# Rotating images by 90 degrees: the first load split in 16 and 112 partitions, in place of a wait before the first store

## The chip, the core and the metric

The kernel runs on one core of a Trainium2 chip. Its time is in microseconds on the device, the median of several executions. The core has 128 partitions of on-chip memory (SBUF), engines that compute, of which this kernel uses VectorE (DVE) and a little of ScalarE (ACT), and 16 DMA engines that move data between SBUF and the chip's main memory (HBM). SyncE (SP) issues all DMAs of this kernel, in the order of the program.

## The reference

```
batch, c, h, w = 32, 3, 256, 256
x = random normal, float32
np.rot90(x, k=-1, axes=(-2, -1))
```

So each of 96 images of 256 x 256 floats is turned by 90 degrees clockwise. Nothing is calculated: 25.17 MB are read and 25.17 MB written, and every element has a new place.

## The kernel before

The 96 images are cut into 12 slabs of 2 MB (8 images each). Each slab has a buffer of its own in SBUF, `units[n]`, of 128 partitions with 2 x 2048 floats (16 KB) on each. So all slabs fit at once, and no load ever waits for a buffer.

*Loads.* The first loop issues all loads, one after the other. Slab 0 comes in two loads of 1 MB (L70): 128 partitions with 8 KB each, that is eight image rows for each partition. Slabs 1 to 10 come in two loads of 1 MB each (L72), which have 64 partitions (every second one) and 16 KB, or 16 image rows, on each. The last slab, number 11, comes in three: 1 MB over all partitions (L64), then 0.25 MB over the first `M = P // 4` = 32 partitions (L65), which the program calls `near_end`, and 0.75 MB over the other 96 (L66). A DMA on SyncE waits, besides its own data, until the DMA eight places before it has landed: eight completion counters take turns.

*Transposes.* The second loop runs over slabs. VectorE's transpose turns blocks of 32 x 32 and writes a slab's result into the buffer of the slab before (`units[n - 1]`), which is free by then; slab 0's result goes to PSUM (`turned0`). Slabs 0 and 11 take two transposes of 128 x 2048 (L80), the others two each (L86).

*Stores.* They are issued in the same loop, on the same SyncE queue, so behind all loads in program order. The result of slab 1 goes out in three stores: 128 KB, which is the first 256 floats of each partition (L89), 896 KB (L92) and 1 MB (L93). Slabs 2 to 11 go out as stores of 2 MB (L95). Slab 0's result is copied by ScalarE from PSUM into the last slab's buffer (L98) and goes out last (L99).

*The order between them.* The first store (L89) has an added dependence on `near_end` (L65): SyncE does not issue it, nor any store behind it, until all loads but the last 96 partitions of the last slab have landed.

Of the kernel before, what the change touches and what calls it, by code (L numbers as in the profile page):

```python
# [1 line left out]

# [4 lines left out]

@with_exitstack
def kernel(
    ctx: ExitStack,
    tc: tile.TileContext,
    x: bass.AP,
    out: bass.AP,
):

    nc = tc.nc
    fp32 = mybir.dt.float32

    B, C, H, W = x.shape  # L40
    P = nc.NUM_PARTITIONS
    RI, RO = 16, 8
    K = H // RI
    I = 2
    Q = P // (K * I)
    n_slabs = B * C // (Q * I)
    last = n_slabs - 1
    F = RO * W
    M = P // 4

    rows_in = x.rearrange("b c h w -> (b c h) w")
    rows_out = out.rearrange("b c h w -> (b c h) w")
    ld8_v = rows_in.rearrange("(n i p r) w -> n p i (r w)", i=I, p=P, r=RO)
    ld16_v = rows_in.rearrange("(n i m r) w -> n i m (r w)", i=I, m=Q * K, r=RI)
    st_v = rows_out.rearrange("(n i p c) w -> n p i (c w)", i=I, p=P, c=RO)

    pools = [ctx.enter_context(tc.tile_pool(name=f"unit{u}", bufs=1)) for u in range(n_slabs)]
    units = [pool.tile([P, I, F], fp32, name=f"u{u}") for u, pool in enumerate(pools)]
    psum = ctx.enter_context(tc.tile_pool(name="psum", bufs=1, space=bass.MemoryType.PSUM))
    turned0 = psum.tile([P, I, F], fp32, name="turned0")  # L60

    for n in range(n_slabs):
        if n == last:
            nc.sync.dma_start(out=units[n][:, 0], in_=ld8_v[n][:, 0])  # L64
            near_end = nc.sync.dma_start(out=units[n][:M, 1], in_=ld8_v[n][:M, 1])  # L65
            nc.sync.dma_start(out=units[n][M:, 1], in_=ld8_v[n][M:, 1])  # L66
            continue
        for i in range(I):
            if n == 0:
                nc.sync.dma_start(out=units[n][:, i], in_=ld8_v[n][:, i])  # L70
            else:
                nc.sync.dma_start(out=units[n][i::I].rearrange("p i f -> p (i f)"), in_=ld16_v[n, i])  # L72

    for n in range(n_slabs):
        t_in, t_out = units[n], units[n - 1] if n else turned0
        if n in (0, last):
            for i in range(I):
                src = t_in[:, i].rearrange("p (r g c) -> p c r g", r=RO, c=RO)
                dst = t_out[:, i].rearrange("p (c g r) -> p c r g", c=RO, r=RO)
                nc.vector.transpose(out=dst[:, :, ::-1, ::-1], in_=src)  # L80
        else:
            src = t_in.rearrange("p i f -> p (i f)").rearrange("p (r g c) -> p c r g", r=RI, c=RO)
            dst = t_out.rearrange("p i (c k r) -> p c r k i", c=RO, r=RI)[:, :, ::-1, ::-1, :]
            for h in range(2):
                cs = slice(h * RO // 2, (h + 1) * RO // 2)
                nc.vector.transpose(out=dst[:, cs], in_=src[:, cs])  # L86

        if n == 1:
            first = nc.sync.dma_start(out=st_v[n][:, 0, :W], in_=t_out[:, 0, :W])  # L89
            tc.add_manual_dep(first.ins, near_end.ins.name, mybir.DependencyInfo(  # L90
                mybir.DependencyClass.Sync, mybir.DependencyReason.DATA), reason="stores after loads")
            nc.sync.dma_start(out=st_v[n][:, 0, W:], in_=t_out[:, 0, W:])  # L92
            nc.sync.dma_start(out=st_v[n][:, 1], in_=t_out[:, 1])  # L93
        elif n:
            nc.sync.dma_start(out=st_v[n], in_=t_out)  # L95

    for i in range(I):
        nc.scalar.copy(out=units[last][:, i], in_=turned0[:, i])  # L98
    nc.sync.dma_start(out=st_v[0], in_=units[last])  # L99


# [1 line left out]
_INS = ['x']  # L103
_OUTS = [((32, 3, 256, 256), 'float32')]


# [23 lines left out]
```

## Time and profile before

| What | us |
|---|---|
| Median of 3 runs (125.41 to 126.25) | 125.93 |
| The profiled execution's own time | 126.25 |
| Its span, from the first to the last instruction | 124.5 |
| VectorE busy, 24 instructions | 93.3 |
| of it the transposes of L86, 20 of 3.945 | 78.0 |
| ScalarE busy, 3 instructions | 5.0 |
| A 1 MB load (L70, L72, L64), median from issue to landing | 19.6 |
| The loads of 0.25 MB (L65) and 0.75 MB (L66), issue to landing | 19.3 and 19.4 |
| The first store of 128 KB (L89), issued at 61.84, issue to landing | 2.9 |
| A 2 MB store, median from issue to landing | 22.0 |
| Packets of all DMAs, as a share of 16 engines' span | 98.1% |

All times that say "at" count from the start of the span. From issue to landing a DMA mostly waits in the DMA engines' queues behind those issued before it. The rows by stretches give, for each stretch of time, how long each computing engine was busy, the mean busy share of the 16 DMA engines and the rate at which their packets moved bytes; a packet counts in the stretch in which it starts, so that single short stretches can show a share above 1. A packet is one contiguous piece of a transfer, 8 KB for most of the transfers here.

### The profile page before, as it was taken

The numbers are of one execution on the slowest core, as the hardware profiler recorded it, in microseconds if no ns is written. First come the engines' busy times: TensorE is split into PE (matmuls) and PEld (weight loads), VectorE is DVE, ScalarE is ACT, GpSimd is POOL, SyncE is SP. The second block draws the span as 40 slices with busy tenths as digits, with TensorE's granted clock in tenths as the row PEclk, the third lists the DMA queues.
The fourth block names the chain that finished last, engine by engine and source line by source line (L and its number), as shares of the span: only waits on it lengthen the run. The fifth ranks groups of instructions, "written<-read, shape, count | busy, mean of one in ns | idle before, by whom it ended". The sixth has DMA issues, their size and how long they took to land.

```text
span 124.5 us, 137 instructions
## 1 busy us (share of the span) xinstructions
DVE 93.3 (75%) x24; ACT 5.0 (4%) x3; POOL 0.2 (0%) x4
## 2 busy tenths in 40 slices
DVE  0199999999999999999999999999999900000000
ACT  0000000000000000000400000000002350000000
POOL 0000000000000000000000000000000000000000
DMA  3999999999999999999999999999999999999995
GB/s 90 427 453 427 427 437 432 421 437 432 421 432 432 427 427 427 442 421 395 219 357 428 429 416 429 413 424 419 421 416 421 421 421 419 421 421 421 421 421 213
DMA packets 5616, 50.33 MB, mean 404 GB/s; under 512 B 624, under 2 KB 752, under 8 KB 880
## 3 DMA queue, kind: packets, MB, share of 16 engines
q1 hardware_dynamic: 5616, 50.33, 98.1%
HBM read 25.17 MB, written 25.17 MB: 404 GB/s over the span
## 4 chain that ended last, share of the span: by engine, by line
DMA 51%; DVE 13%; issue 10%; DVEq 6%; ACT 1%
DMA u<-in_x_dram 51%; DVE u L86 13%; DVEq L125 6%; ACT u L98 1%; DVE u L80 0%
## 5 line engine op out<-in xcount | busy, mean ns | idle before, releaser
L86 DVE STREAM_TRANSPOSE u<-u 128x2048 f32<-128x2048 f32 x20 | 78.0, 3945 | 0.3
L80 DVE STREAM_TRANSPOSE turned<-u 128x2048 f32<-128x2048 f32 x2 | 7.6, 3826 | 5.8 <-DMA u<-in_x_dram 5.8
L80 DVE STREAM_TRANSPOSE u<-u 128x2048 f32<-128x2048 f32 x2 | 7.7, 3953 | 0.0
L98 ACT COPY u<-turned 128x2048 f32<-128x2048 f32 x2 | 3.7, 1866 | 36.1 <-DVE u L80 36.1
L98 ACT ACT_TABLE_LOAD x1 | 1.3, 1283 | 60.2 <-DMA u<-in_x_dram 60.2
L114 POOL MEMSET const-bfloat16-1.0<- 128x1 bf16 x1 | 0.1, 102 | 0.0
L114 POOL MEMSET const-uint8-127<- 128x1 uint8 x1 | 0.1, 102 | 0.0
L114 POOL MEMSET const-float32-1.0<- 128x1 f32 x1 | 0.1, 99 | 0.0
L114 POOL MEMSET const-float32-0.0<- 128x1 f32 x1 | 0.1, 98 | 0.2 <-issue 0.2
## 6 DMA issues: line engine op xcount, KB each, us to landing
u<-in_x_dram SPq DMA_DIRECT2D x23, 1024.0 KB, 19.6
out_dram<-u SPq DMA_DIRECT2D x11, 2048.0 KB, 22.0
out_dram<-u SPq DMA_DIRECT2D x1, 1024.0 KB, 6.4
out_dram<-u SPq DMA_DIRECT2D x1, 896.0 KB, 4.4
u<-in_x_dram SPq DMA_DIRECT2D x1, 768.0 KB, 19.4
u<-in_x_dram SPq DMA_DIRECT2D x1, 256.0 KB, 19.3
out_dram<-u SPq DMA_DIRECT2D x1, 128.0 KB, 2.9
```

The lines of the kernel that those rows point to most:

```text
L80: nc.vector.transpose(out=dst[:, :, ::-1, ::-1], in_=src)
L86: nc.vector.transpose(out=dst[:, cs], in_=src[:, cs])
L98: nc.scalar.copy(out=units[last][:, i], in_=turned0[:, i])
L114: nc = _bacc.Bacc("TRN2", target_bir_lowering=False, num_devices=1)
L125: with _tile.TileContext(nc) as tc:
```

## The change

Three edits. The first load of 1 MB (slab 0's first half) becomes two loads, one of the first 16 partitions (128 KB) and one of the other 112 (896 KB). The last slab's three loads become a single one of 2 MB over all partitions, and the name `near_end` goes. The first store loses its added dependence, so it waits only for its own data and for the DMA eight places before it. Loads are 24 in place of 25. The three stores of slab 1, the transposes and the copies stay as they are.

```
-    M = P // 4
+    FIRST = 16
...
         if n == last:
-            nc.sync.dma_start(out=units[n][:, 0], in_=ld8_v[n][:, 0])
-            near_end = nc.sync.dma_start(out=units[n][:M, 1], in_=ld8_v[n][:M, 1])
-            nc.sync.dma_start(out=units[n][M:, 1], in_=ld8_v[n][M:, 1])
+            nc.sync.dma_start(out=units[n], in_=ld8_v[n])
             continue
         for i in range(I):
             if n == 0:
-                nc.sync.dma_start(out=units[n][:, i], in_=ld8_v[n][:, i])
+                for a, b in ((0, FIRST), (FIRST, P)) if i == 0 else ((0, P),):
+                    nc.sync.dma_start(out=units[n][a:b, i], in_=ld8_v[n][a:b, i])
...
         if n == 1:
-            first = nc.sync.dma_start(out=st_v[n][:, 0, :W], in_=t_out[:, 0, :W])
-            tc.add_manual_dep(first.ins, near_end.ins.name, mybir.DependencyInfo(
-                mybir.DependencyClass.Sync, mybir.DependencyReason.DATA), reason="stores after loads")
+            nc.sync.dma_start(out=st_v[n][:, 0, :W], in_=t_out[:, 0, :W])
             nc.sync.dma_start(out=st_v[n][:, 0, W:], in_=t_out[:, 0, W:])
```

## The prediction, made before the changed kernel ran

> **What bounds the kernel now.** I read the page's slices first, because they say which resource is never idle.
>
> ```profile
> DVE  0199999999999999999999999999999900000000
> ACT  0000000000000000000400000000002350000000
> ...
> DMA  3999999999999999999999999999999999999995
> GB/s 90 427 453 427 427 437 432 421 437 432 421 432 432 427 427 427 442 421 395 219 357 428 429 416 429 413 424 419 421 416 421 421 421 419 421 421 421 421 421 213
> ```
>
> A slice is 3.11 us. The DMA engines are busy from the second slice to the last, so the end is set by how fast 50.33 MB pass through them. VectorE, busy for 93.3 us, stops in slice 30, and ScalarE soon after. Three places stand out: the start (90 GB/s), the end (213), and a hole in slices 18 to 20 (395, 219, 357) where the DMA row still says 9. Against 427 the hole lacks 32 + 208 + 70 GB/s over 3.11 us each, 0.96 MB, or 2.3 us.
>
> Second, the chain of waits, which gives the pace of the loads:
>
> ```profile
> 0.73 5.01 DMA u<-in_x_dram
> ...
> 5.76 19.55 DMA u<-in_x_dram
> ...
> 25.32 19.56 DMA u<-in_x_dram
> ...
> 44.91 19.32 DMA u<-in_x_dram
> ```
>
> Each piece is one load from issue to landing, and it is issued when the load eight places before it has landed. So 19.56 us is the time of eight loads of 1 MB: 2.445 us each. The last piece holds six whole loads (the last five of L72 and that of L64) and the loads of 0.25 and 0.75 MB (L65, L66): 7 MB, which should take 17.11 us. It took 19.32, 2.2 us too much. That is the hole, seen from another side.
>
> Third, rows of half a microsecond around the start and the hole. The columns after the stretch are VectorE, ScalarE and GpSimd busy (and instructions), a clock that plays no part, the DMA share and GB/s.
>
> ```profile
> 1.50:2.00 0.50, 0.00 (x0) 0.00 (x0) 0.00 (x0) 1.00 0.91 131
> 2.00:2.50 0.50, 0.00 (x0) 0.00 (x0) 0.00 (x0) 1.00 0.19 49
> 2.50:3.00 0.50, 0.00 (x0) 0.00 (x0) 0.00 (x0) 1.00 0.92 311
> ...
> 58.00:58.50 0.50, 0.50 (x1) 0.00 (x0) 0.00 (x0) 1.00 0.99 410
> ...
> 59.50:60.00 0.50, 0.50 (x1) 0.00 (x0) 0.00 (x0) 1.00 0.93 197
> 60.00:60.50 0.50, 0.47 (x2) 0.31 (x1) 0.00 (x0) 1.00 1.17 213
> 60.50:61.00 0.50, 0.50 (x1) 0.50 (x1) 0.00 (x0) 1.00 0.95 197
> 61.00:61.50 0.50, 0.50 (x1) 0.47 (x1) 0.00 (x0) 1.00 0.95 262
> 61.50:62.00 0.50, 0.50 (x1) 0.00 (x0) 0.00 (x0) 1.00 1.00 262
> 62.00:62.50 0.50, 0.50 (x1) 0.00 (x0) 0.00 (x0) 1.00 1.15 295
> ```
>
> Share and rate give the time of one 8 KB packet, 16 x share x 8.192 / GB/s. At 58.0 it is 16 x 0.99 x 8.192 / 410 = 0.32 us. In the hole it is 0.62, 0.72, 0.63, 0.475, 0.50 and 0.51 us. So the engines are not idle in the hole: they carry slow packets, and these are exactly the packets of L65 (32 partitions, two packets for each of 16 engines, 0.62 and a like one before it) and L66 (96 partitions, six packets; the five rows from 60.0 have a mean of 0.57). Eight packets at 0.31 would be 2.5 us; these eight took about 2 x 0.63 + 6 x 0.57 = 4.7 us. The excess is 2.2 us for the third time. Loads over fewer than 128 of consecutive partitions are slow here, and the wait is not what makes the hole.
>
> Last, SyncE's waits, for the wait itself:
>
> ```profile
> SPq L89 <- DMA u<-in_x_dram: 16.5, 1, 16.5
> ```
>
> **The change, part by part.** *The wait at L89 goes.* The first store was issued at 61.84, after 16.5 us of waiting, and behind it on SyncE stood all other stores. Without the wait it goes out when the load eight places ahead has landed, near 47 us, its data having been ready since about 21 us (first L86 pair at 13.36 plus 7.8). But its packets join the engines' queues behind the loads, which are never empty: over 62.0 to 64.0 the share is 1.15, 0.72, 0.80 and 1.26, mean 0.98. A queue full of loads is the cover; I put the gain of the wait at 0, at most 0.1 us. Were the cover gone, about 1 us from issue to first byte (0.73 to some 1.75 at the start) would show. If instead stores passed ahead of loads, late loads would cost nothing until VectorE held up the stores: the last store is issued at 101.36 and lands 22.2 us later, of which it needs about 5 itself (2.1 MB at 421 GB/s), so there are 17 us to spare, and 14 for the one before it (issued at 99.5, landing near 118.6).
>
> *L64, L65 and L66 become one 2 MB load.* It covers 128 partitions in 8 KB rows, as the 2 MB stores do, which run at 421. It ends the slow packets: -2.2 us. Bounds: -1.6 if part of the hole belongs to the turn from loads to stores (the 128 KB store in 1 KB rows stays, at 62.8 to 63.5, rows of 180 and 234 GB/s), -2.3 by the slices. VectorE's L80 on the last slab now waits for 2 MB instead of 1, but starts at 91.69, some 30 us after landing. Two issues of 0.35 us less on SyncE lie under 19 us of queue.
>
> *The first 1 MB load becomes 16 + 112 partitions.* This brings slow packets to the start, where nothing covers them: every later packet of each engine queues behind. Before, 131 GB/s in 0.5 us is eight packets begun, 49 is three, 311 is 19: half the engines begin at about 1.75 and the others only after 2.5. The load landed at 5.74, though 1.75 + 8 x 0.31 + 0.5 for landing (the store's data end by 123.0, its landing is at 123.6) is 4.7: starting costs 1.0 us. After, the first load has one packet for each engine. No row shows a load of 16 partitions; 128 take 0.31 a packet, 32 take 0.62, half of 32 might double again: 1.24, with 0.31 as the other end. I take 1.24, since the nearest row is the 32 one and the fall is steep, and 0.3 more for the slow first touch that the first packets show. The load of 112 has seven packets an engine, between 0.31 (128) and 0.57 (96): 0.43, the middle, makes 3.0. In all 1.75 + 1.24 + 0.3 + 3.0 + 0.5 = 6.8, less 0.15 since all engines may begin a little earlier with so small a first load: 6.65, +0.9 us on the first landing. Low end: full-rate packets and all engines awake at 1.65, 1.65 + 0.9 + 7 x 0.31 + 0.5 = 5.2, -0.5. High end: 1.75 + 1.24 + 0.7 + 7 x 0.57 + 0.5 = 8.2, +2.4. VectorE starts later by the same amount, inside its 14 us of room; the added issue of about 0.35 us on SyncE delays the second load's issue, which has more than 4 us of queue ahead of it.
>
> The Trainium skill, "SBUF — State Buffer", section "Door 1: The DMA port swizzle", says that a DMA's rate depends on how many of 16 ports its partitions reach, and by its table 32 partitions from 0 reach eight, 16 reach four, which speaks against the new split as much as against the old one. The 0.62 us of the 32-partition packets agrees with it. An estimate from that page's table, seven consecutive partitions an engine, is 1.24 for the 16 and up to 2.8 for the 112, which would put the cost at the start at 0.7 and the time at 124.4.
>
> **Sum.** -2.2 + 0.9 = -1.3 us. The profiled execution took 126.25 (its span of 124.5 and 1.75 around it), and would take 124.95; the median of the runs is 0.3 lower, so 125.93 - 1.3 = 124.6.
>
> **Rivals.** *The start costs nothing or gains* (the small load's slow packet hides under the first touch, and 112 partitions run like 128): -2.2 - 0.5 to -2.2 + 0.1, 123.2 to 123.8. For it: first packets were slow anyway. Against: 32 and 96 were both slow on all engines. *The start takes back all*: costs of 1.6 to 2.6, 125.3 to 126.3; for it, the 96-partition mean of 0.57. *Slower*: the packets of the new first loads go at the worst row of the hole, 0.72, or 1.44 for those of 16 partitions: 1.75 + 1.44 + 0.7 + 7 x 0.72 + 0.5 = 9.4, +3.7, against -2.2: 127.4. It decides when a 112-partition packet takes more than about 0.7 us; only one row of the hole was that slow, with two loads mixed in it. *The wait was the hole*, and the change gives 2.2 for its removal: the same number for that part, but the busy share speaks against it.
>
> **Chances.** The forecast (123.9 to 125.3) 0.62, a free start 0.14, all taken back 0.14, slower 0.10. Of this kernel's time 1% is 1.26 us, about what a measurement can tell from no change, and the bound of "faster" is 124.67, almost at my number: of the forecast, half falls on each side. Faster 0.31 + 0.14 = 0.45, same 0.31 + 0.14 = 0.45, slower 0.10. Range 123.6 to 126.3: it leaves out part of the free start and the slower case.
>
> **What would show it.** Steps right: no stretch under 400 GB/s between the loads' steady pace and the first store; the first store issued near 47 us and landing much later than 2.9 us after; the first VectorE transpose near 6.6 instead of 5.76, and rows near 200 to 300 GB/s before it; the stores of 2 MB unchanged. Wrong: a hole that stays at 59 us with one 2 MB load (then it was not the narrow loads), a first transpose before 5.8 or after 8, or gaps in the DMA share while stores wait for VectorE.

## The result, and the profile after

The changed kernel takes 124.58 us (median of 6, 124.45 to 124.70) against 125.80 for the kernel before (6 runs beside it, 125.41 to 126.25): a ratio of 0.9899, 95% interval 0.9875 to 0.9923. That is 1.0% faster, 0.02 us from the forecast. The next sections show that two terms behind that number were wrong and largely cancelled.

The page of the changed kernel, slices of 3.07 us:

```profile
span 122.8 us, 136 instructions
...
DMA  3999999999999999999999999999999999999994
GB/s 80 304 448 427 432 427 432 432 432 427 427 427 427 427 427 427 427 427 387 424 418 425 427 427 427 430 427 427 430 427 430 430 427 430 427 427 427 430 430 205
```

Of the hole in the middle (395, 219, 357) the last two slices are gone (424 and 418 now). The first stays, at 387, so hardly any of it was due to the narrow loads, though the prediction counted it with them; and its sign of being right, no stretch under 400, is not quite met. A new hole stands in the second slice (304 where 427 stood). A third difference was not forecast: the stores' slices, at 421 for most of the second half before, are at 427 to 430.

SyncE's timeline of the changed kernel: start, duration, what.

```profile
41.03 0.40 SPq L63 DMA_DIRECT2D u<-in_x_dram  x1
43.54 0.38 SPq L87 DMA_DIRECT2D out_dram<-u  x1
45.97 0.35 SPq L88 DMA_DIRECT2D out_dram<-u  x1
```

The first store now goes out at 43.5 in place of 61.84, and lands 20.2 us later in place of 2.9: it waits in the engines' queues instead of in SyncE's, as forecast. It goes out earlier than the 47 of the prediction, which counted eight places back in the old order of DMAs; in the new order the load eight places ahead of the first store is one that comes two megabytes sooner. The run without the wait, with the old loads, has it at 47.46.

The start of the changed kernel, in stretches with the same columns as before (share and GB/s at the end):

```profile
1.50:2.00 0.50, 0.00 (x0) 0.00 (x0) 0.00 (x0) 1.00 1.17 262
2.00:2.50 0.50, 0.00 (x0) 0.00 (x0) 0.00 (x0) 1.00 0.21 33
2.50:3.00 0.50, 0.00 (x0) 0.00 (x0) 0.00 (x0) 1.00 0.56 131
...
3.50:6.00 2.50, 0.00 (x0) 0.00 (x0) 0.00 (x0) 1.00 1.04 318
```

All 16 packets of the 16-partition load begin at once (262 GB/s in 0.5 us is sixteen) and take 16 x 1.17 x 8.192 / 262 = 0.59 us. When they end, from about 2.34 on, most engines have nothing to do for a while: two packets begin in the half microsecond up to 2.5 and eight in the one after, although the second load was issued only 0.45 us after the first. From 3.5 on its packets run at 16 x 1.04 x 8.192 / 318 = 0.43 us. The first transpose starts at 6.9 us in place of 5.8.

### The profile page after: what moved, and what is told of

It reads as the page before. It is cut to its first block, busy times and chain, and to the rows that moved or that the text cites. A ratio compares the mean times of both kernels' runs of the same rounds, so it can differ in the third digit from the quotient of the medians.

```text
span 122.8 us, 136 instructions
## 1 busy us (share of the span) xinstructions
DVE 93.3 (76%) x24; ACT 5.0 (4%) x3; POOL 0.2 (0%) x4
## 4 chain that ended last, share of the span: by engine, by line
DMA 52%; DVE 16%; issue 10%; DVEq 3%; ACT 2%; SPq 0%
DMA u<-in_x_dram 36%; DMA out_dram<-u 16%; DVE u L84 13%; DVE u L78 3%; DVEq L121 3%; ACT u L94 2%; SPq L68 0%; SPq L88 0%
## 6 DMA issues: line engine op xcount, KB each, us to landing
out_dram<-u SPq DMA_DIRECT2D x1, 128.0 KB, 20.2
```

## The experiments

Each ratio is to runs of the kernel before on the same chip, with its 95% interval. The two runs with strided partitions and with 8 x 16 partitions rest on two executions each, the others on four to twelve.

| Run | Median, us | Ratio |
|---|---|---|
| no added wait | 125.19 | 0.9956 (0.9943 to 0.9969) |
| whole loads at the end, wait kept | 124.28 | 0.9885 (0.9869 to 0.9900) |
| neither split nor wait | 123.78 | 0.9848 (0.9831 to 0.9866) |
| before, plus the split of the first load | 126.56 | 1.0060 (1.0041 to 1.0079) |
| last MB in 4 x 32 consecutive partitions | 125.85 | 0.9981 (0.9958 to 1.0003) |
| last MB in 4 x 32 strided partitions | 123.82 | 0.9835 (0.9798 to 0.9871) |
| last MB in 8 x 16 consecutive partitions | 127.99 | 1.0166 (1.0128 to 1.0204) |
| first MB in even and odd halves | 124.66 | 0.9912 (0.9881 to 0.9943) |
| wait for slab 10 | 123.88 | 0.9855 (0.9835 to 0.9875) |
| wait for slab 8 | 124.03 | 0.9867 (0.9847 to 0.9887) |
| one first store | 123.95 | 0.9862 (0.9845 to 0.9879) |
| halves from two queues | 124.29 | 0.9881 (0.9862 to 0.9901) |

### The change taken apart

The first four runs divide the change: the wait alone, the narrow loads at the end alone, both of these without the new split, and the new split alone. The kernel before had 125.73 beside them (11 runs).

Without the added wait:

```
-            first = nc.sync.dma_start(out=st_v[n][:, 0, :W], in_=t_out[:, 0, :W])
-            tc.add_manual_dep(first.ins, near_end.ins.name, ...)
+            nc.sync.dma_start(out=st_v[n][:, 0, :W], in_=t_out[:, 0, :W])
```

> The kernel before without the added dependence of the first store; the last slab still comes in loads of 128, 32 and 96 partitions. Theory (narrow loads make the hole, the wait costs nothing): 125.7 to 125.9, within 0.1 of before; the first store is issued near 47 us, and the packets around 60 us still take 0.5 to 0.7 us. Rival (the wait makes the hole): the hole goes, 123.6.

It took 125.19: 0.54 us less, neither the nothing of my theory nor the 2.2 of the rival.

With whole loads at the end, the wait moved to the first of them:

```
-            nc.sync.dma_start(out=units[n][:, 0], in_=ld8_v[n][:, 0])
-            near_end = nc.sync.dma_start(out=units[n][:M, 1], in_=ld8_v[n][:M, 1])
-            nc.sync.dma_start(out=units[n][M:, 1], in_=ld8_v[n][M:, 1])
+            near_end = nc.sync.dma_start(out=units[n][:, 0], in_=ld8_v[n][:, 0])
+            nc.sync.dma_start(out=units[n][:, 1], in_=ld8_v[n][:, 1])
```

> The kernel before with its wait, but the last slab in two loads of 1 MB over all 128 partitions; the first store waits for the first of them, so it is issued with 1 MB, about 2.4 us, of loads still queued. Theory: the hole goes although the wait stays, 125.8 - 2.2 = 123.6. Rival (the wait makes the hole): 125.8, with a stretch near 62 us in which the DMA share falls.

124.28, 1.45 us less. The hole closes with the wait in place, so the theory holds on what makes it, and the size is off. The hole and the stores, first of the kernel before, then of the run without the wait, then of this one:

```profile
59.00:63.00 4.00, 3.96 (x2) 1.28 (x1) 0.00 (x0) 1.00 1.00 229
66.00:119.00 53.00, 33.30 (x9) 3.73 (x2) 0.00 (x0) 1.00 1.01 421
```

```profile
59.00:63.00 4.00, 3.96 (x2) 1.28 (x1) 0.00 (x0) 1.00 0.97 238
66.00:119.00 53.00, 33.19 (x9) 3.73 (x2) 0.00 (x0) 1.00 1.01 428
```

```profile
59.00:63.00 4.00, 3.96 (x2) 1.28 (x1) 0.00 (x0) 1.00 1.00 407
66.00:119.00 53.00, 33.13 (x9) 3.73 (x2) 0.00 (x0) 1.00 1.01 421
```

The reader is to see two independent effects. The first row of each pair follows the narrow loads: 229 and 238 with them, 407 without. The second follows the wait: 421 with it, 428 without, at the same busy share of 1.01. The wait leaves no engine idle; it goes with slower store packets, 16 x 1.01 x 8.192 / 421 = 0.314 us against 0.309, for the whole second half. These are traces of single executions, and the one of the kernel before is the slowest of its six (126.25, with a median of 125.80): 421 in place of 428 over 53 us is 0.87 us, the gap between the two profiled executions is 126.25 - 125.34 = 0.91, and between the medians it is 0.54.

Without the split of the first load, that is, the change without its new part:

```
-                for a, b in ((0, FIRST), (FIRST, P)) if i == 0 else ((0, P),):
-                    nc.sync.dma_start(out=units[n][a:b, i], in_=ld8_v[n][a:b, i])
+                nc.sync.dma_start(out=units[n][:, i], in_=ld8_v[n][:, i])
```

> The kernel after without the split of the first load (128 partitions in one load again). Theory: the first load lands near 5.7 us in place of 6.8, and the time is 124.58 - 1.0 = 123.6, as in the run with whole loads and the wait. Rival (the split of the first load gains at the start, and the landing of the whole first megabyte does not matter): 124.6 or more.

123.78, the best of all versions here and 0.80 under the changed kernel: the new split costs that. And the kernel before with that same split added, the reverse of the last diff:

> The kernel before, unchanged at its end, with the first load split in 16 and 112 partitions. Theory: 125.8 + 1.0 = 126.8, the slow stretch near 60 us as before and 1.0 us later. Rival (some of the end's gain comes from the start, through the order in which the queues run): not additive, under 126.3.

126.56, 0.83 more. Each part was thus measured beside two states of the others, and hardly depends on them: the split costs 0.80 or 0.83, the narrow loads 1.41 without the wait (125.19 to 123.78) and 1.45 with it, the wait 0.54 with narrow loads and 0.50 with whole ones (124.28 to 123.78). So the change is about -0.54 - 1.41 + 0.80 = -1.15, where -1.22 was measured beside other runs of the kernel before.

### What makes a load slow

Three runs start from the version without split and wait. They bring the last slab in as 1 MB over all partitions and cut its second megabyte in different ways.

```
+            for q in range(4):
+                nc.sync.dma_start(out=units[n][32 * q:32 * (q + 1), 1], in_=ld8_v[n][32 * q:32 * (q + 1), 1])
```

> The kernel without either split (123.78), but the last megabyte of the last slab comes in four loads of 32 consecutive partitions, two 8 KB packets for each of 16 engines. Theory (a load over 32 consecutive partitions takes 0.62 us a packet wherever it stands): eight packets of 0.62 in place of 0.31, 123.8 + 2.5 = 126.3. Rival (it is the unequal pair 32 + 96, or the load after it, that is slow): under 125.

```
+            for q in range(4):
+                nc.sync.dma_start(out=units[n][q::4, 1], in_=ld8_v[n][q::4, 1])
```

> As the run with four loads of 32 consecutive partitions, but each of the four takes every fourth partition (0, 4, 8, ... and so on): as many loads, packets and bytes, spread over all 128 partitions. Theory (what counts is where the partitions lie): packets of 0.31 us, 123.8 to 124.1. Rival (what counts is how few partitions a load has): packets of 0.62, 126.3.

```
+            for q in range(8):
+                nc.sync.dma_start(out=units[n][16 * q:16 * (q + 1), 1], in_=ld8_v[n][16 * q:16 * (q + 1), 1])
```

> The kernel without either split, but the last megabyte comes in eight loads of 16 consecutive partitions, one packet for each engine. My prediction's step (half of 32 partitions doubles the packet time once more): 1.24 us a packet, 123.8 + 7.4 = 131.2. Rival (the 16-partition load of the changed kernel showed packets of 0.58 us at the start, so 16 partitions are as slow as 32 and no slower): 123.8 + 2.2 = 126.0.

They took 125.85, 123.82 and 127.99; consecutive quarters cost 2.07 us, a little less than the 2.5 of the theory. Rows from the middle of each split megabyte, in the same order (consecutive quarters, strided quarters, sixteens):

```profile
60.00:63.00 3.00, 2.96 (x2) 1.28 (x1) 0.00 (x0) 1.00 1.03 224
```

```profile
59.00:59.50 0.50, 0.50 (x1) 0.00 (x0) 0.00 (x0) 1.00 1.11 459
59.50:60.00 0.50, 0.50 (x1) 0.41 (x1) 0.00 (x0) 1.00 0.87 361
```

```profile
60.00:63.00 3.00, 2.96 (x2) 1.27 (x1) 0.00 (x0) 1.00 1.08 161
```

These are packets of 0.60, 0.32 (at 410 GB/s over the two rows) and 0.88 us. Quarters of the same size, number and packet length differ by almost two, and all that differs is which partitions they name and, tied to that by the layout, which rows of HBM they read. So it is not small loads, nor a load count, that cost: it is a run of neighbours. The strided quarters cost nothing against the whole load (123.82 and 123.78).

Whether the neighbours that matter are the partitions of SBUF or the rows of HBM is not shown: a consecutive quarter reads one piece of 256 KB, a strided one 32 rows that lie 32 KB apart, and no run parts the two. One sign speaks for the partitions. The rows in which the run of consecutive quarters passes through its second, third and fourth quarter:

```profile
60.50:61.00 0.50, 0.50 (x1) 0.50 (x1) 0.00 (x0) 1.00 1.20 246
61.00:61.50 0.50, 0.50 (x1) 0.50 (x1) 0.00 (x0) 1.00 0.79 180
61.50:62.00 0.50, 0.50 (x1) 0.00 (x1) 0.00 (x0) 1.00 0.96 229
62.00:62.50 0.50, 0.50 (x1) 0.00 (x0) 0.00 (x0) 1.00 0.98 213
62.50:63.00 0.50, 0.50 (x1) 0.00 (x0) 0.00 (x0) 1.00 1.02 213
```

The packets take 0.64, 0.58, 0.55, 0.60 and 0.63 us. They are faster only around 61.5, where, by the count of packets, the queues pass from the second quarter (partitions 32 to 63) to the third (64 to 95), and not near 62.5, at the next change of quarters, though the step in HBM is the same.

Eight loads of 16 partitions are slower than loads of 32, but not twice as slow: neither my 1.24 nor the rival's 0.58 holds. The one load of 16 at the start of the changed kernel took 0.59 us a packet; why eight in a row take 0.88 was not looked into.

### Where the wait stands

The run with whole loads, with the wait on another load:

```
+                ld = nc.sync.dma_start(out=units[n][i::I].rearrange("p i f -> p (i f)"), in_=ld16_v[n, i])
+                if (n, i) == (10, 1):
+                    near_end = ld
```

> The run with whole loads and the wait (124.28), with the first store waiting for the second load of slab 10 in place of the first megabyte of slab 11: it goes out near 57.0 in place of 59.6, with 2 MB of loads still queued. What is open: why the wait costs about 0.5 us although no DMA engine idles; store packets take 314 ns with it and 309 without. Theory (the stores' issues come in a burst behind the wait): still a burst of seven, so packets near 314 and 124.1 to 124.4. Rival (only a wait that ends close to the end of the loads costs): 309 and 123.8.

and with `(8, 1)` in the condition:

> As the run above, with the first store waiting for the second load of slab 8, near 47.3, which is 2.4 us later than it would go out by itself. Theory and rival: no burst and a wait far from the end, packets of 309 ns and 123.7 to 123.9. If it is the added wait as such, whenever it ends: 314 and 124.3.

123.88 and 124.03, both within 0.25 of the version without any wait; 124.03 lies between the two expectations (up to 123.9, and 124.3), and its stores, at 428, decide for the first. The run with the wait for slab 10 on SyncE and in its stores:

```profile
57.17 0.35 SPq L90 DMA_DIRECT2D out_dram<-u  x1
57.62 0.38 SPq L93 DMA_DIRECT2D out_dram<-u  x1
58.05 0.42 SPq L94 DMA_DIRECT2D out_dram<-u  x1
...
66.00:119.00 53.00, 33.30 (x9) 3.73 (x2) 0.00 (x0) 1.00 1.01 428
```

The stores still leave in a burst, 0.45 us apart, and still run at 428. So neither the burst nor the wait as such slows them; in these traces a wait that ends at 59.6 or later, with 1 MB or less of loads queued, does, and one that ends at 57.2 with 2 MB does not. What in the chip keeps the packets at 0.314 us for 50 us afterwards stays open; in the kernel before with the split added the stores even began at 428 (70 to 95 us) and fell to 422 (95 to 119).

### The turn to the stores, and the start

Three more runs looked for time in the version without split and wait. With one store of 2 MB for slab 1 in place of three:

```
-            nc.sync.dma_start(out=st_v[n][:, 0, :W], in_=t_out[:, 0, :W])
-            nc.sync.dma_start(out=st_v[n][:, 0, W:], in_=t_out[:, 0, W:])
-            nc.sync.dma_start(out=st_v[n][:, 1], in_=t_out[:, 1])
+            nc.sync.dma_start(out=st_v[n], in_=t_out)
```

> The kernel without either split (123.78), with the three first stores of slab 1 (128 KB in 1 KB rows, 896 KB, 1 MB) as one of 2 MB like the others. In the run without either split the packets between 60 and 62 us took 0.34 to 0.39 us in place of 0.31, while some engines were already on 1 KB packets. Theory (the 1 KB packets beside the last loads cost this): 123.3 to 123.6. Rival (the turn from loads to stores costs it, whatever the stores): 123.7 to 123.9.

123.95, so the small store is not what the turn costs. From 59 to 63 us the rate was 379 GB/s, against 373 with three stores. What does cost there stays open.

With the first megabyte in two halves, first from SyncE alone, then, on top of the single store, the odd half from ScalarE:

```
+                for q in range(2 if i == 0 else 1):
+                    s = slice(q, None, 2) if i == 0 else slice(None)
+                    nc.sync.dma_start(out=units[n][s, i], in_=ld8_v[n][s, i])
```

> The kernel without either split (123.78), with the first 1 MB load in two loads of 64 partitions each, the even ones and the odd ones, in place of one of 128. Theory (partitions spread over all 128 go at full rate; half the engines begin 0.75 us late because the first load's descriptors are written for them after those of the others, so a load half as long wakes them sooner): the first load lands 0.1 to 0.4 us sooner, 123.4 to 123.7. Rival (the late half is late for another reason, or the second issue of 0.4 us costs as much): 123.8 to 124.2.

```
+                    nc.sync.dma_start(out=units[n][0::2, i], in_=ld8_v[n][0::2, i])
+                    nc.scalar.dma_start(out=units[n][1::2, i], in_=ld8_v[n][1::2, i])
```

> As the run with one first store, with the first megabyte in two loads of 64 partitions, the even ones issued by SyncE and the odd ones by ScalarE at the same time. In the run with two halves from SyncE alone all engines began together, but at 2.05 to 2.26 us, and the time came out between 124.1 and 126.1. Theory (what was lost there is the second issue on SyncE): the first load lands before 5.5 and the time is 0.1 to 0.3 under the run with one first store. Rival (a start in halves costs, whoever issues it): the same or more, and again wide apart from execution to execution.

124.66 and 124.29, worse than 123.78 and 123.95. The run with two halves from SyncE at its start:

```profile
1.50:2.00 0.50, 0.00 (x0) 0.00 (x0) 0.00 (x0) 1.00 0.00 0
2.00:2.50 0.50, 0.00 (x0) 0.00 (x0) 0.00 (x0) 1.00 1.98 262
2.50:3.00 0.50, 0.00 (x0) 0.00 (x0) 0.00 (x0) 1.00 0.21 66
```

All engines do begin together, but only after 2.0, and their first packets take 16 x 1.98 x 8.192 / 262 = 0.99 us. With ScalarE issuing one half it is the same: no packet begins before 2.0, and the first take 0.94 us. The first transpose starts at 6.0 in both runs, against 5.6 with one whole load. That all engines begin together gains nothing when they begin later than the first half of them did (1.75) and each then takes about 1 us for its first packet. So a load half as long did not wake the late engines sooner, and why they are late with a whole load stays open. The 124.66 is the middle of 12 executions from 124.06 to 126.12; why these lie so far apart was not looked into.

## Why the prediction was right, by its steps

*The hole is slow packets of loads over few consecutive partitions, not idleness.* Shown: it closes with the wait kept, and it comes back or not with the choice of partitions (and of the HBM rows tied to them).

*The wait is worth 0, at most 0.1.* This step failed. It is worth 0.54 (125.73 to 125.19). The reasoning looked for idle DMA engines at 62 to 64 us, and rightly found none; it did not ask whether the stores behind the wait ran as fast as they could. The page showed 421 for most slices of stores and mostly 427 to 437 for loads, and I took 421 for what stores do. The rival that the wait is the hole falls too: the gain lies in the 50 us after it.

*Whole loads at the end gain 2.2 (1.6 to 2.3).* The mechanism was right and the term too large: 1.41 to 1.45 was measured, below the low bound. The three derivations that agreed on 2.2 shared one mistake: they compared the hole with a steady stream, but in every run here the turn from loads to stores leaves something there. In the run with whole loads and the wait, 59 to 63 us still stood at 407, so the rise was (407 - 229) x 4 us = 0.71 MB, 1.7 us at 428. The first derivation also counted the slice of 395, which stayed. And all three were read from one execution, the slowest of the kernel before: from it to the profiled execution with whole loads the gain is 126.25 - 124.47 = 1.78, near those 1.7, where the medians give 1.45.

*The split of the first load costs 0.9.* 0.80 and 0.83 were measured, and the first transpose came at 6.9 (the step had 6.65 for the landing, which was 6.77). The 112 partitions at 0.43 us a packet, taken halfway between the rows of 128 and 96, were right: 0.43. The 16 partitions at 1.24 + 0.3 were not: 0.59, followed by about 0.9 us (what 1.75, 0.59, 7 x 0.43 and 0.5 leave of 6.77) in which the second load's first packets come late and slowly, which I had not seen. The term was right by luck, since these two errors cancelled.

*VectorE's late start costs nothing.* Right: it starts 1.1 us later, and the last store, issued at 102.52, still queues behind others until 121.9. *The 2 MB load runs at full rate:* right, 424 in its slice. (VectorE ends in slice 31, not in 30, as the prediction read it; nothing rests on that.)

The forecast of -1.3 was thus -2.2 + 0.9 and turned out as -1.41 - 0.54 + 0.80. That it came within 0.1 us of the measured -1.22 is luck in part: the narrow loads were taken 0.8 too high, and the wait, taken as nothing, gave 0.54 of that back.

The Trainium skill, "SBUF — State Buffer", section "Door 1: The DMA port swizzle", ties the rate to the ports that a load's partitions reach. The two kinds of quarters agree with it: 224 GB/s against 410. By its table 16 consecutive partitions reach four of 16 ports, an estimate of a quarter of the full 430, 108 GB/s; the sixteens moved 161, and there the measurement decides. That estimate is for one such load alone, while eight stood in a row here, and whether neighbouring ones moved side by side was not looked into. The prediction's 2.8 for the 112 comes without its working; seven packets of 0.43 are 3.0.

## What to carry to other kernels

Split a load by partitions only if the parts are strided over all of them; neighbouring partitions cost a factor of 1.4 (112 of them) to 2.8 (16) in every packet, and where nothing covers it (the first load, a queue that never runs dry) that is time. When an engine's busy share is full, compare its rate per packet between stages as well: a wait can cost in the pace after it without leaving any gap. And a term read from a hole should be set against the hole that stays, not against a steady stream.

## What was not expected of the hardware

- Time of an 8 KB packet by the partitions of its load: 128 consecutive 0.31 us, 112 consecutive 0.43, 96 about 0.57 (the first of its six with another load's packets among them; 0.48 to 0.51 from 61.0 to 62.5 us), 32 about 0.60, 16 about 0.88 in a row of eight loads and 0.59 for one alone at the start, and 32 strided by four 0.32.
- Stores ran at 421 GB/s after a wait that ended with 1 MB or less of loads queued, and at 428 after one with 2 MB or more or without a wait. In the kernel before with the split added they fell from 428 to 422 only on the way.
- A DMA of one packet per engine starts all 16 engines at 1.75 us, where one of eight packets each starts half of them 0.75 us later; of the next load's packets only two then begin before 2.5 us.
